# The first two pieces of x and the first weight granule's halves: two transfers instead of four

## The chip, the cores and the metric

The kernel runs on one core of one Trainium2 chip. The metric is device time in microseconds for one execution of the whole program. Times are medians over several executions; the profile is of one further execution, with its own time.

A core has several engines that run side by side, each with its own instruction queue worked off in order: PE (TensorE, matrix products; PEld is its weight load), DVE (VectorE), ACT (ScalarE), POOL (GpSimd) and SP (SyncE, here the queue that issues most transfers from memory). [...] The transfers themselves run on 16 DMA engines.

## The reference

The input is 512 tokens of 1024 channels in float32. Two layers each apply a gated feed-forward block, a mixer and a second feed-forward block, and a last normalization follows:

```python
for l in range(DEPTH):                                   # DEPTH = 2
    x = x + 0.5 * swiglu(rms_norm(x, ffn1_norm[l]), ffn1_w_in[l], ffn1_w_out[l])
    x = x + mixer(rms_norm(x, mix_norm[l]), ...)         # neighbourhood attention + 2-D DFT, gated
    x = x + 0.5 * swiglu(rms_norm(x, ffn2_norm[l]), ffn2_w_in[l], ffn2_w_out[l])
return rms_norm(x, final_norm)
```

with `swiglu(x, w_in, w_out) = (silu(g) * u) @ w_out` and `g, u` the two halves of `x @ w_in`; `w_in` is 1024 x 5632, `w_out` 2816 x 1024. Only the very first steps of the first `swiglu` matter for this change.

## The kernel before, in words

**Products in three parts.** Every float32 operand is split into a rounded high part and the low rest. For the weights ScalarE writes `whi` (L210, or L205 with the sign turned) and VectorE the rest `wlo` (L213, L206). For x they are `xh` (L353) and `xl` (L354). A product is then three matmuls per 128 rows of depth: `whi,xh` (L539), `whi,xl` (L540) and `wlo,xh` (L542). The root mean square is not needed for that: only the gain `gn` is multiplied into x; the division comes later. Most large products further on use Strassen's scheme of seven products, for which sums and differences of operand blocks are made.

**Weights come in granules.** A granule is 128 x 1024 float32, 512 KB. A list of items, one per granule and use, sets their order. `Item.load` issues the transfer on SP (L155) into a `raw` buffer, `Item.prep` makes `whi` and `wlo` of it; `ws.fetch` and `ws.next` keep loads and preparations ahead of the products. In the feed-forward stages the `raw` buffers are a pool of nine that are taken in turn. When a stage ends, the pool is closed, and the next stage's tiles take over its memory, each as soon as its last user there is done. Some loads are sums that POOL's queue adds in flight (L165).

**The start.** The first 256 gate and 256 up columns are computed plainly (the `cl` products): four granules, each of two 128-row pieces of depth, against the eight pieces of transposed x (`xt`, 128 channels x 512 tokens, 256 KB each). Per piece there are four output banks and so twelve matmuls. The first granule is loaded and prepared in two halves of 256 KB, so that PE can begin on the first piece of x with the first half. Before that, ten matmuls on zeros (`warm`, L143) run on PE. Each piece of x is also multiplied by the gain into `xr` (L428, two halves of 256 tokens), and halves are combined (L726 and later) for the Strassen products behind.

**What sets the order.** SP's order at the start is written out by hand (a block in which SP keeps program order): first piece of x, first weight halves, second piece of x, then x in pairs of pieces, each with the next granule. The order on PE, VectorE and ScalarE in this stretch is set by the framework's planner from dependences and its own estimates, apart from the combinations, which are by hand. POOL's first transfer of the mixer is `ch` (L1145), into memory of the closed `raw` pool.

Of the kernel before, what the change touches and what calls it, by code (L numbers as in the profile page):

```python
# [9 lines left out]
F32 = mybir.dt.float32  # L10
# [4 lines left out]
AF = mybir.ActivationFunctionType  # L15
ALU = mybir.AluOpType
AX = mybir.AxisListType

P = 128
D = 1024  # L20
T = 512
# [28 lines left out]
def _granules():  # L50

    names, at = [], {}

    def put(*key):
        at[key] = len(names)
        names.append(key)

    for l in range(L):
        for w in (1, 2):
            s = (l, w)  # L60
            for g in range(4):
                put(s, *(("cl", g) if s == (0, 1) else ("h" + "abcd"[g], 0, 0)))
            for j in range(NB):
                for g in range(2):
                    put(s, "a", j, g)
                for g in range(2):
                    put(s, "c", j, g)
                    put(s, "d", j, g)
                for g in range(2):
                    put(s, "b", j, g)  # L70
            for q in "abcd":
                for c in range(3):
                    for g in range(2):
                        put(s, "o" + q, c, g)
            if w == 1:
                s = (l, 0)
                for q in "abcd":
                    for g in range(2):
                        put(s, "u" + q, 0, g)
                for name, n in (("qk", 8), ("f", 5)):  # L80
                    for g in range(n):
                        put(s, name, g)
                for i in range(2):
                    for g in range(2):
                        put(s, "n", i, g)
                    for q in "acdb":
                        for g in range(2):
                            put(s, "g" + q, i, g)
                for q in "acdb":
                    for g in range(2):  # L90
                        put(s, "w" + q, 0, g)
    return names, at


GRAN, GRAN_AT = _granules()
# [1 line left out]

@with_exitstack
def encoder_kernel(
    ctx: ExitStack, tc: tile.TileContext, xin, xtr, wst, gains, gfin, gbias, bias_in, dft, chan, ident_in, rot, out  # L100
):
    nc = tc.nc
    V, S, G, PE = nc.vector, nc.scalar, nc.gpsimd, nc.tensor
# [11 lines left out]
    def nm(s):  # L115
        uid[0] += 1
        return f"{s}_{uid[0]}"

    def slot(dt=F32, s="k", shape=(4, 256)):
        return kp.tile([P, *shape], dt, tag="k", name=nm(s), bufs=23)  # L120
# [14 lines left out]
    ident = cp.tile([P, P], F32, tag="ident", name="ident")  # L135
# [31 lines left out]
    class Item:  # L167
# [30 lines left out]
        def prep(self, nxt):  # L198
            n = self.raw.n
            hi = wp.tile([P, 1024], F32R, tag="whi", name=nm("whi"), bufs=3)[:, 0:n]  # L200
            lo = wp.tile([P, 1024], F32R, tag="wlo", name=nm("wlo"), bufs=3)[:, 0:n]
            t = self.raw.t
            self.summed()
            if self.neg:
                S.activation(hi, t, AF.Copy, scale=-1.0)  # L205
                self.last = V.scalar_tensor_tensor(lo, t, -1.0, hi.bitcast(F32), ALU.mult, ALU.subtract)  # L206
            else:
                for c in range(0, n, n // self.parts):
                    cs = slice(c, c + n // self.parts)
                    S.activation(hi[:, cs], t[:, cs], AF.Copy)  # L210
                    if nxt and not nxt.twice:
                        nxt.summed()
                    self.last = V.tensor_tensor(lo[:, cs], t[:, cs], hi[:, cs].bitcast(F32), ALU.subtract)  # L213
            if self.then:
                G.dma_start(out=t, in_=wst[GRAN_AT[self.then]][:, 0:n], accum_op=ALU.add)
            self.out = (hi, lo)
# [123 lines left out]
    ws = Stream()  # L340
# [1706 lines left out]
    swap_pools(0, False)  # L2047
    norm = Norm(0)
    with tc.manual_schedule(engines={mybir.EngineType.SP}):
        for kts in ((0,), (1,), (2, 3), (4, 5), (6, 7)):  # L2050
            src = slot(F32, "xt", (2, T))[:, 0 : len(kts), :]
            nc.sync.dma_start(out=src, in_=xtr[:, kts[0] : kts[-1] + 1, :])
            ws.fetch(kts[-1] // 2 + 1)
            for k, kt in enumerate(kts):
                norm.given(*divmod(kt, 4), src[:, k, :])
        ws.fetch(6)
        for tb in range(TB):
            nc.sync.dma_start(out=x[:, tb, :], in_=xin[:, tb, :])
        nc.sync.dma_start(out=ident, in_=ident_in)
        ws.fetch(10)  # L2060
    for l in range(L):
        nxt = Norm(3 * l + 1)
        stage_ffn(norm, nxt, False)
        norm, nxt = nxt, Norm(3 * l + 2)
        stage_mixer(l, norm, nxt)
        norm, nxt = nxt, Norm(3 * l + 3)
        stage_ffn(norm, nxt, l == L - 1)
        norm = nxt
# [184 lines left out]
```

## Time and profile before

| | us |
|---|---|
| median of 3 runs | 1838.45 |
| lowest, highest | 1838.39, 1839.38 |
| the profiled execution's own time | 1837.46 |
| its span, first to last instruction | 1835.7 |
| PE busy in the span | 1823.8 |
| VectorE busy | 1607.2 |
| ScalarE busy | 1306.2 |

A row of a timeline reads: start in us from the span's start, time in us, engine, line, operation, output<-inputs, the number of instructions merged in the row, and in brackets how long the engine had been idle before and what ended that. "SPq" is the time that SP's queue spends on issuing a transfer, not the transfer's. In the chain of waits each row has start, time and what the end of the program depended on. In the table of stretches each engine has its busy time and instruction count; the last three columns are PE's granted clock, the mean busy share of the DMA engines and GB/s.

### The profile page before, as it was taken

The numbers are of one execution on the slowest core, as the hardware profiler recorded it, in microseconds if no ns is written. First come the engines' busy times: TensorE is split into PE (matmuls) and PEld (weight loads), VectorE is DVE, ScalarE is ACT, GpSimd is POOL, SyncE is SP. The second block draws the span as 40 slices with busy tenths as digits, with TensorE's granted clock in tenths as the row PEclk, the third lists the DMA queues.
The fourth block names the chain that finished last, engine by engine and source line by source line (L and its number), as shares of the span: only waits on it lengthen the run. The fifth ranks groups of instructions, "written<-read, shape, count | busy, mean of one in ns | idle before, by whom it ended". The sixth has DMA issues, their size and how long they took to land.

```text
span 1835.7 us, 24504 instructions
## 1 busy us (share of the span) xinstructions
PE 1823.8 (99%) x8766; PEld 1509.6 (82%) x8766; DVE 1607.2 (88%) x1952; ACT 1306.2 (71%) x1771; POOL 179.2 (10%) x219
## 2 busy tenths in 40 slices
PE   9999999999999999999999999999999999999998
PEld 7888888887878888888888888888888788888876
DVE  7878899878989988889998888998789899887898
ACT  6777875667576777787667777766776776777865
POOL 0001011110111010101010100101001111100010
PEclk9999999999999999999999999999999999999999
DMA  9898798963997789879878987998639876988795
GB/s 303 223 237 225 184 274 272 225 175 116 277 221 193 166 233 242 208 201 281 249 194 212 240 212 197 274 296 186 179 134 264 227 190 183 238 212 223 202 272 162
DMA packets 206387, 403.75 MB, mean 220 GB/s; under 512 B 108733, under 2 KB 108893, under 8 KB 206265
## 3 DMA queue, kind: packets, MB, share of 16 engines
q1 hardware_dynamic: 176536, 300.52, 51.0%
q0 software_dynamic: 29296, 101.12, 30.5%
q8 instruction: 69, 1.13, 0.3%
q10 hardware_dynamic: 432, 0.55, 0.1%
q14 instruction: 54, 0.43, 0.1%
HBM read 370.67 MB, written 2.11 MB: 203 GB/s over the span
## 4 chain that ended last, share of the span: by engine, by line
PE 89%; DVE 3%; DMA 3%; issue 2%; ACT 2%; POOL 0%; SPq 0%; DVEq 0%; ACTq 0%; POOLq 0%
PE A L539 10%; PE A L540 10%; PE A L542 10%; PE o L540 7%; PE o L539 7%; PE o L542 7%; PE B L542 5%; PE B L540 5%; PE B L539 5%; PE ps L344 3%; PE ps L345 3%; PE ps L346 2%; PE C L540 2%; PE C L539 2%; PE C L542 2%
## 5 line engine op out<-in xcount | busy, mean ns | idle before, releaser
L213 DVE TENSOR_TENSOR wlo<-raw,whi 128x1024 fp32r<-128x1024 f32 (+1 forms) x534 | 630.8, 1190 | 166.3 <-ACT whi L210 165.8
L210 ACT ACTIVATE whi<-raw 128x1024 fp32r<-128x1024 f32 (+1 forms) x534 | 546.2, 1033 | 265.4 <-DVE raw L182 70.7
L165 POOL DMA_DIRECT2D raw<-in_wst_dram x170 | 148.6, 900 | 1301.7 <-DMA raw<-in_wst_dram 467.6
L182 DVE TENSOR_TENSOR raw<-raw,raw 128x1024 f32<-128x1024 f32 (+1 forms) x148 | 176.1, 1190 | 2.0
L540 PE MATMUL A<-whi,xl 128*128 128x512 f32 x400 | 155.7, 389 | 0.0
L539 PE MATMUL A<-whi,xh 128*128 128x512 f32 x400 | 155.7, 389 | 0.0
L394 ACT ACTIVATE at<-zt 128x1024 uint16<-128x1024 uint16 (+2 forms) x96 | 110.2, 1165 | 12.0 <-DMA zt<-zs 12.0
L542 PE MATMUL A<-wlo,xh 128*128 128x512 f32 x400 | 115.0, 389 | 0.0
L205 ACT ACTIVATE whi<-raw 128x1024 fp32r<-128x1024 f32 (+1 forms) x83 | 85.6, 1036 | 38.7 <-issue 11.3
L206 DVE SCALAR_TENSOR_TENSOR wlo<-raw,whi 128x1024 fp32r<-128x1024 f32 (+1 forms) x83 | 98.6, 1192 | 11.5 <-ACT whi L205 11.5
L542 PEld LDWEIGHTS A<-wlo,xh 128*128 128x128 f32 x400 | 75.1, 188 | 15.6
L540 PEld LDWEIGHTS A<-whi,xl 128*128 128x128 f32 x400 | 75.1, 188 | 15.4
L539 PEld LDWEIGHTS A<-whi,xh 128*128 128x128 f32 x400 | 75.1, 188 | 15.4
L539 PE MATMUL B<-whi,xh 128*128 128x512 f32 x208 | 81.4, 391 | 1.2 <-ACT whi L210 1.1
L540 PE MATMUL B<-whi,xl 128*128 128x512 f32 x208 | 81.0, 390 | 0.0
L540 PE MATMUL C<-whi,xl 128*128 128x512 f32 x208 | 81.0, 389 | 0.0
L539 PE MATMUL C<-whi,xh 128*128 128x512 f32 x208 | 81.0, 389 | 0.0
L794 ACT ACTIVATE th<-sn,rh 128x512 f32<-128x512 f32 x80 | 54.9, 715 | 36.3 <-DVE sn L631 35.5
L375 ACT ACTIVATE zs<-th 128x1024 uint16<-128x1024 uint16 x80 | 79.5, 1043 | 0.9 <-DVE th L801 0.9
L626 ACT ACTIVATE sn<-A 128x512 f32<-128x512 f32 x104 | 59.0, 586 | 27.5 <-PE A L542 27.2
L542 PE MATMUL B<-wlo,xh 128*128 128x512 f32 x208 | 60.2, 391 | 0.2
L542 PE MATMUL C<-wlo,xh 128*128 128x512 f32 x208 | 60.1, 390 | 0.0
(451 smaller groups left out, 4618.7 us busy)
## 6 DMA issues: line engine op xcount, KB each, us to landing
raw<-in_wst_dram SPq DMA_DIRECT2D x468, 512.0 KB, 6.3
raw<-in_wst_dram POOLq DMA_DIRECT2D x180, 512.0 KB, 8.1
bm<-in_bias_dram SPq DMA_DIRECT2D x16, 512.0 KB, 6.2
raw<-in_wst_dram SPq DMA_DIRECT2D x30, 256.0 KB, 5.1
vs<-v SPq DMA_DIRECT2D x24, 128.0 KB, 5.8
x<-in_xin_dram SPq DMA_DIRECT2D x4, 512.0 KB, 10.2
raw<-in_wst_dram POOLq DMA_DIRECT2D x8, 256.0 KB, 8.4
dft<-in_dft_dram POOLq DMA_DIRECT2D x8, 256.0 KB, 6.7
```

Source lines behind the costliest of these rows:

```text
L165: G.dma_start(out=self.t, in_=wst[GRAN_AT[self.plus]][:, 0 : self.n], accum_op=ALU.add)
L182: V.tensor_tensor(self.raw.t, self.raw.t, self.add.t, ALU.add)
L205: S.activation(hi, t, AF.Copy, scale=-1.0)
L206: self.last = V.scalar_tensor_tensor(lo, t, -1.0, hi.bitcast(F32), ALU.mult, ALU.subtract)
L210: S.activation(hi[:, cs], t[:, cs], AF.Copy)
L213: self.last = V.tensor_tensor(lo[:, cs], t[:, cs], hi[:, cs].bitcast(F32), ALU.subtract)
L375: S.activation(s[:, h], words[:, h], AF.Copy)
L394: S.activation(to[:, w], t[:, w], AF.Copy)
L539: PE.matmul(ps, lh, rh, start=start, stop=False, skip_group_check=again)
L540: PE.matmul(ps, ll, rh, start=False, stop=False, skip_group_check=again)
L542: PE.matmul(ps, lh, rl, start=False, stop=stop, skip_group_check=again)
L626: last_snap[0] = S.activation(t[:, b, :], ps[b], AF.Copy)
```

## The change

The host lays the first two pieces of x and the two halves of the first granule side by side in a new input `head` (128 x 2 x 2 x 512: per piece, x and then its half of the weights). Two transfers of 512 KB bring them into two `xt` tiles. The first item's `raw` is then no buffer of the pool but a list of the two weight parts of these tiles, and `prep` takes its source from there. The input `xtr` holds the other six pieces.

```diff
-                    S.activation(hi[:, cs], t[:, cs], AF.Copy)
+                    src = t[c // T] if isinstance(t, list) else t[:, cs]
+                    S.activation(hi[:, cs], src, AF.Copy)
                     if nxt and not nxt.twice:
                         nxt.summed()
-                    self.last = V.tensor_tensor(lo[:, cs], t[:, cs], hi[:, cs].bitcast(F32), ALU.subtract)
+                    self.last = V.tensor_tensor(lo[:, cs], src, hi[:, cs].bitcast(F32), ALU.subtract)
...
     with tc.manual_schedule(engines={mybir.EngineType.SP}):
-        for kts in ((0,), (1,), (2, 3), (4, 5), (6, 7)):
-            src = slot(F32, "xt", (2, T))[:, 0 : len(kts), :]
-            nc.sync.dma_start(out=src, in_=xtr[:, kts[0] : kts[-1] + 1, :])
+        begin = [slot(F32, "xt", (2, T)) for _ in range(2)]
+        ws.items[0].raw.t = [t[:, 1, :] for t in begin]
+        for kt, t in enumerate(begin):
+            nc.sync.dma_start(out=t, in_=head[:, kt])
+            norm.given(0, kt, t[:, 0, :])
+        ws.fetch(1)
+        for kts in ((2, 3), (4, 5), (6, 7)):
+            src = slot(F32, "xt", (2, T))
+            nc.sync.dma_start(out=src, in_=xtr[:, kts[0] - 2 : kts[-1] - 1, :])
             ws.fetch(kts[-1] // 2 + 1)
             for k, kt in enumerate(kts):
                 norm.given(*divmod(kt, 4), src[:, k, :])
...
+    head = np.stack([xtr[:, 0:2], wst[GRAN_AT[(0, 1), "cl", 0]].reshape(P, 2, T)], axis=2)
+    xtr = np.ascontiguousarray(xtr[:, 2:])
```

How the instructions stand on the engines before and after follows for three places. Lines of the changed kernel lie one to seven further down (L354 is now the `xh` line, L211 `whi`, L214 `wlo`, L355 `xl`, L429 `xr`).

SP's first transfers before, from the program's start on; `xt` are pieces of x, `raw` is weights:

```order
L2052 DMA xt_102<-in_xtr_dram 128x512
L155 DMA raw_104<-in_wst_dram 128x512 x2
L2052 DMA xt_115<-in_xtr_dram 128x512
L2052 DMA xt_121<-in_xtr_dram 128x1024
L155 DMA raw_123<-in_wst_dram 128x1024
L2052 DMA xt_133<-in_xtr_dram 128x1024
```

And in the changed kernel:

```order
L2054 DMA xt_102<-in_head_dram 128x1024
L2054 DMA xt_103<-in_head_dram 128x1024
L2059 DMA xt_118<-in_xtr_dram 128x1024
L155 DMA raw_120<-in_wst_dram 128x1024
L2059 DMA xt_130<-in_xtr_dram 128x1024
```

The two weight halves and the single pieces are gone as transfers of their own; everything behind stands two places earlier.

VectorE from the low rest of the third granule's weights to that of the first Strassen weights, before (`wlo_227` is of the fourth `cl` granule, L726 a combination of `xr` halves):

```order
L213 TENSOR_TENSOR wlo_199<-raw_135,whi_198 128x1024
L726 TENSOR_TENSOR xr_111<-xr_111,xr_113 128x1024
L354 SCALAR_TENSOR_TENSOR xl_138<-xt_149,gn,xh_137 128x512
L428 TENSOR_SCALAR xr_141<-xt_149,gn 128x256
L428 TENSOR_SCALAR xr_143<-xt_149,gn 128x256
L354 SCALAR_TENSOR_TENSOR xl_138<-xt_149,gn,xh_137 128x512
L428 TENSOR_SCALAR xr_141<-xt_149,gn 128x256
L428 TENSOR_SCALAR xr_143<-xt_149,gn 128x256
L213 TENSOR_TENSOR wlo_227<-raw_151,whi_226 128x1024
L206 SCALAR_TENSOR_TENSOR wlo_255<-raw_161,whi_254 128x1024
```

And in the changed kernel, where `wlo_224` is of the fourth granule and the combination is L727:

```order
L214 TENSOR_TENSOR wlo_196<-raw_132,whi_195 128x1024
L429 TENSOR_SCALAR xr_138<-xt_146,gn 128x256
L355 SCALAR_TENSOR_TENSOR xl_135<-xt_146,gn,xh_134 128x512
L429 TENSOR_SCALAR xr_140<-xt_146,gn 128x256
L355 SCALAR_TENSOR_TENSOR xl_135<-xt_146,gn,xh_134 128x512
L429 TENSOR_SCALAR xr_138<-xt_146,gn 128x256
L429 TENSOR_SCALAR xr_140<-xt_146,gn 128x256
L214 TENSOR_TENSOR wlo_224<-raw_148,whi_223 128x1024
L727 TENSOR_TENSOR xr_109<-xr_109,xr_111 128x1024
L206 SCALAR_TENSOR_TENSOR wlo_252<-raw_158,whi_251 128x1024
```

The combination moved from ahead of the last x pieces to behind the fourth granule's low rest.

PE's first products of the second piece of x in the changed kernel (L540 is now `whi,xh`, L541 `whi,xl`; `cl` are the four output banks):

```order
L540 MATMUL cl_179<-whi_183,xh_105 128x512
L540 MATMUL cl_180<-whi_183,xh_105 128x512
L541 MATMUL cl_179<-whi_183,xl_106 128x512
L541 MATMUL cl_180<-whi_183,xl_106 128x512
L540 MATMUL cl_181<-whi_183,xh_105 128x512
L541 MATMUL cl_181<-whi_183,xl_106 128x512
```

Before, `whi,xh` and `whi,xl` alternated from the first bank on; now two `whi,xh` come first, for the first piece as well.

More of the change, by code (lines that the diff above doesn't have):

```diff
@@ L99, in encoder_kernel @@
 def encoder_kernel(
-    ctx: ExitStack, tc: tile.TileContext, xin, xtr, wst, gains, gfin, gbias, bias_in, dft, chan, ident_in, rot, out
+    ctx: ExitStack, tc: tile.TileContext, xin, head, xtr, wst, gains, gfin, gbias, bias_in, dft, chan, ident_in, rot, out
 ):
@@ L2240 @@
     nc = _bacc.Bacc("TRN2", target_bir_lowering=False, num_devices=1)
-    arrays = dict(xin=xin, xtr=xtr, wst=wst, gains=gains, gfin=gfin, gbias=gbias, bias=bias, dft=dft, chan=chan, ident=ident, rot=rot)
+    arrays = dict(xin=xin, head=head, xtr=xtr, wst=wst, gains=gains, gfin=gfin, gbias=gbias, bias=bias, dft=dft, chan=chan, ident=ident, rot=rot)
     arrays = {f"in_{k}_dram": v for k, v in arrays.items()}
```

## The prediction

> **What bounds the kernel now.** I read the page first, then the chain of waits, then the first 30 us engine by engine, because the transfers that change are the first ones of the program.
>
> ```profile
> span 1835.7 us, 24504 instructions
> PE 1823.8 (99%) x8766; PEld 1509.6 (82%) x8766; DVE 1607.2 (88%) x1952; ACT 1306.2 (71%) x1771; POOL 179.2 (10%) x219
> ```
>
> PE is busy for all but 11.9 us (1835.7 - 1823.8) of the span, so a change that removes no PE work can win only where PE waits or runs slowly. The chain of waits over the first 40 us shows who sets the pace there (start us, us, what):
>
> ```profile
> 2.61 6.61 DMA xt<-in_xtr_dram
> 9.24 0.88 DVE xr L428 x3
> ...
> 21.12 0.73 PE cl L542 x2
> ...
> 39.54 0.23 PE B L539
> ```
>
> First a transfer of x, then an unbroken run of VectorE, and from 21.12 us on PE itself. The timeline of PE (start us, us, what) shows what that costs PE:
>
> ```profile
> 1.19 4.45 PE L143 MATMUL ps<-warm 128*128 128x512 bf16 x10 [1.19 <-DVE ones L139]
> 5.14 0.92 PE L539 MATMUL cl<-whi,xh 128*128 128x512 f32 x1
> 5.87 0.63 PE L540 MATMUL cl<-whi,xl 128*128 128x512 f32 x1
> ...
> 6.72 0.42 PE L540 MATMUL cl<-whi,xl 128*128 128x512 f32 x1
> 6.98 0.40 PE L539 MATMUL cl<-whi,xh 128*128 128x512 f32 x1
> ...
> 8.83 0.39 PE L539 MATMUL cl<-whi,xh 128*128 128x512 f32 x1
> 9.18 0.50 PE L540 MATMUL cl<-whi,xl 128*128 128x512 f32 x1
> 9.51 0.39 PE L539 MATMUL cl<-whi,xh 128*128 128x512 f32 x1
> ...
> 11.81 0.39 PE L539 MATMUL cl<-whi,xh 128*128 128x512 f32 x1
> ...
> 20.65 0.39 PE L540 MATMUL cl<-whi,xl 128*128 128x512 f32 x1
> 21.12 0.73 PE L542 MATMUL cl<-wlo,xh 128*128 128x512 f32 x2
> 21.69 0.39 PE L539 MATMUL cl<-whi,xh 128*128 128x512 f32 x1
> ...
> 25.78 0.39 PE L539 MATMUL cl<-whi,xh 128*128 128x512 f32 x1
> ...
> 28.50 0.39 PE L539 MATMUL A<-whi,xh 128*128 128x512 f32 x1
> ```
>
> Starts matter here, not durations, since matmuls overlap. Undisturbed, 12 matmuls take 28.50 - 25.78 = 2.72 us, 0.227 each. From 5.87 to 6.72 they start 0.43 apart (two steps), at about half that rate; from 6.98 at the full one. Twelve matmuls use one piece of x (128 rows) with its half of the first weight granule. The second twelve (8.83 to 11.81) take 2.98 us, 0.26 more than 2.72: 9.18 and 9.51 came late. Then PE loses 0.36 us more, around 21.12: 0.47 instead of 0.23 before it, 0.57 instead of 0.45 behind. Three things can be won: 0.26, 0.36, and part of the half-rate start. ScalarE and VectorE show what those waited for:
>
> ```profile
> 3.85 0.72 ACT L353 ACTIVATE xh<-xt,gn 128x512 fp32r<-128x512 f32 x1 [1.17 <-DMA gn<-in_gains_dram]
> 4.48 0.61 ACT L210 ACTIVATE whi<-raw 128x512 fp32r<-128x512 f32 x1
> 5.85 0.63 ACT L210 ACTIVATE whi<-raw 128x512 fp32r<-128x512 f32 x1 [0.76 <-DMA raw<-in_wst_dram]
> 7.61 0.73 ACT L353 ACTIVATE xh<-xt,gn 128x512 fp32r<-128x512 f32 x1 [1.13 <-DMA xt<-in_xtr_dram]
> ```
>
> ```profile
> 4.61 0.75 DVE L354 SCALAR_TENSOR_TENSOR xl<-xt,gn,xh 128x512 fp32r<-128x512 f32 x1
> 5.27 0.69 DVE L213 TENSOR_TENSOR wlo<-raw,whi 128x512 fp32r<-128x512 f32 x1
> ...
> 7.61 0.62 DVE L428 TENSOR_SCALAR xr<-xt,gn 128x256 f32<-128x256 f32 x2 [0.40 <-DMA xt<-in_xtr_dram]
> 8.37 0.75 DVE L354 SCALAR_TENSOR_TENSOR xl<-xt,gn,xh 128x512 fp32r<-128x512 f32 x1
> ...
> 16.33 1.22 DVE L726 TENSOR_TENSOR xr<-xr,xr 128x1024 f32<-128x1024 f32 x1
> 17.47 0.75 DVE L354 SCALAR_TENSOR_TENSOR xl<-xt,gn,xh 128x512 fp32r<-128x512 f32 x1
> ...
> 19.84 1.22 DVE L213 TENSOR_TENSOR wlo<-raw,whi 128x1024 fp32r<-128x1024 f32 x1
> ```
>
> The first piece of x waits for the gains at 3.85, so it is itself in by then. Its weight half is in by 4.48 (ScalarE goes on without idle time), the second weight half at 5.85, the second piece of x at 7.61. The 9.18 matmul waited for the xl of 8.37 to 9.12, the 21.12 matmul for the wlo of 19.84 to 21.06.
>
> **The change, part by part.** (1) *Two issues fewer.* Four issues of 256 KB become two of 512 KB:
>
> ```profile
> 0.74 0.40 SPq L2052 DMA_DIRECT2D xt<-in_xtr_dram  x1
> 1.21 0.89 SPq L155 DMA_DIRECT2D raw<-in_wst_dram  x2
> ```
>
> An issue takes about 0.47 us of the queue (0.74 to 1.21), so everything from the third transfer on is issued about 0.9 us earlier. Bytes stay the same, and the stretches show what the DMA engines made of them (columns end with DMA share and GB/s):
>
> ```profile
> 2.00:4.00 2.00, 2.00 (x6) 0.76 (x5) 0.15 (x1) 0.82 (x3) 0.00 (x0) 1.00 0.89 301
> 4.00:6.00 2.00, 2.00 (x6) 1.06 (x5) 1.82 (x4) 1.24 (x3) 0.00 (x0) 1.00 0.78 210
> 8.00:10.00 2.00, 2.00 (x10) 1.35 (x9) 1.74 (x5) 1.10 (x3) 0.00 (x0) 1.00 1.01 399
> ```
>
> In the 4 to 6 us stretch they are idle 22% of the time. Earlier issues may fill that or not; no row says.
>
> (2) *The first pair is usable only when all of it is in.* Bounds: 3.8 us (the 524 KB and 25 KB of gains at 301 GB/s from 2.00 on) and 4.48 (the same bytes were in by then). I take 4.3, near the row that stands for the same bytes. ScalarE then makes xh (0.63 to the next start) and whi (0.61), so the first product can start at about 5.59 instead of 5.14. What hides this are the warm-up matmuls, which hold PE until 5.64 (1.19 + 4.45); the second product at 5.87 less 0.43 puts the first one's real start at 5.44. The delay is 0.15 us at half rate, worth 0.08 us of full-rate work (0.227/0.43). Bounds: nothing, and 0.17 (landing at 4.48). Without that cover it would be 0.45. VectorE's xl and wlo move by the same 0.45, to 5.06 and 5.72, and are needed only at the third and the ninth product.
>
> (3) *The second pair lands together.* At the earliest 4.3 + 524 KB at 399 GB/s = 5.6 us, at the latest 7.61, when the same bytes had landed; no row lies nearer to either, so I take the middle, 6.6. xh and whi are then done by 7.9 (0.63 + 0.61), xl by 8.11 (8.37 + 0.75 was 1.51 behind the landing), wlo by 8.71, all before PE comes to them at 8.91 (8.83 + 0.08). Even with 7.61 whi is done at 8.85 and xl at 9.12; the new order puts two whi,xh matmuls ahead of the first that needs xl, so that one stands at 8.91 + 0.45 = 9.36. The second twelve then take 2.72 us: 0.26 won.
>
> (4) *VectorE's order moves.* The combination of two xr halves (L726, 1.14 us from 16.33 to 17.47) now stands behind the wlo that PE awaited at 21.12. On the other side the second wlo half (0.6 to the next start: 1.81 - 1.22 for such a one and a long one, below at 309.96) comes behind the second xl instead of ahead. If the second pair lands at 7.61, VectorE starts the third piece at 9.63 instead of 9.24, and the wlo ends at 21.06 - 1.14 + 0.39 = 20.31; with 6.6 it is 1.0 us earlier still. PE comes for it at 20.65 + 0.23 - 0.18 = 20.70. So the 0.36 us go (bounds: 0 and 0.36). The moved combination feeds the product that starts at 39.54; it has over 15 us.
>
> (5) *The first granule takes no raw buffer*, which shifts the rotation of nine by one in this stage. At the entry of the mixer the ch transfer on POOL takes over the first buffer's place, and everything behind it on POOL waits:
>
> ```profile
> 307.63 1.22 DVE L213 TENSOR_TENSOR wlo<-raw,whi 128x1024 fp32r<-128x1024 f32 x1
> ...
> 309.96 1.81 DVE L213 TENSOR_TENSOR wlo<-raw,whi 128x1024 fp32r<-128x1024 f32 x2
> ```
>
> ```profile
> 309.14 0.57 POOL L1145 DMA_DIRECT2D ch<-in_chan_dram  x1 [20.65 <-DVE wlo L213]
> 312.15 0.85 POOL L165 DMA_DIRECT2D raw<-in_wst_dram  x1 [2.43 <-DMA raw<-in_wst_dram]
> ```
>
> Its releaser becomes the first of the pair at 309.96 (a 128x512, 0.69 us, done at 310.65), so ch goes out near 310.95 and is issued by 311.5. The next on POOL waits until 312.15 for its own data: nothing lost, with 0.63 us to spare. Beyond that, each us late would hold up POOL's loads by as much.
>
> Sum: +0.08 - 0.26 - 0.36 = **-0.54 us**; bounds -0.09 and -0.62. The profiled execution took 1837.46 us (span 1835.7 and 1.76 around it), which gives 1836.9. That execution lies 0.99 below the median of 1838.45 (runs from 1838.39 to 1839.38), so for the median I write **1837.9**. More than 0.62 cannot come from here, however early the data: before 5.44 PE is held by the warm-ups.
>
> [...]
>
> **Rivals.** *Slower: the clock rises later.* PE is at half rate up to 6.72, 5.6 us after its first warm-up. If the first pair lands after 4.35 (5.64 less the 1.29 it needs to become a product), PE stands idle between warm-ups and products, and the full rate may come later. Each us at half rate costs 0.47 us (1 - 0.227/0.43). The delay is bounded by nothing and by another 5.6 us; half of it costs 1.3, all of it 2.6. Time: 1837.9 + 1.3 = 1839.2, at most 1840.5. For it: my landing of 4.3 stands right at the edge. Against: a gap would be some tenths in over 4 us of work, and the gap before 21.12 left the rate as it was. Chance 0.12.
>
> [...]
>
> *The second pair lands late.* From 7.7 us on each us counts in full: at 8.5 the second twelve start at 9.79 instead of 8.91, the sum is +0.34, the time 1838.8. For it: the sag to 210 GB/s. Against: the same bytes had landed at 7.61 behind two more issues. Chance 0.08.
>
> *The gain is lost later: no change, 1838.45.* PE has 1% of idle time behind the start, and a wait there that isn't tied to PE's own progress would swallow half a us. Against: POOL's and SP's waits there end with VectorE's work, as above, and move along. Chance 0.10.
>
> *More than the sum*, by later waits that also shrink: 1836.5 or less; the 11.9 us of idle PE are the cap. Chance 0.05.
>
> **How the numbers follow.** The forecast keeps 0.65. Its own range is 1837.4 to 1838.9: the bounds of the sum and the spread of 0.99 us among the runs of before. With the clock and the late landing mostly in, I give 1836.9 to 1839.6 for 8 in 10. A change counts as faster or slower beyond 0.2%, 3.7 us, about what a measurement of this kernel can tell from no change. Every case above but its far tail lies inside: the clock rival ends at +2.1, the larger gain would have to take a third of all idle PE time. So 0.03 faster, 0.94 the same, 0.03 slower.
>
> **What would show it.** PE's timeline: first product near 5.6, half rate ending between 6.7 and 7.0, the second twelve without the 0.35 us steps, no gap at the first wlo pair near 20.7, and the A product starting near 27.96 instead of 28.50. ScalarE: the first xh at 4.3 (wrong if above 4.48), the second between 5.6 and 7.6. VectorE: no idle time from the third piece on, the L726 step (now L727) behind the fourth wlo. POOL: ch near 311, the raw transfer behind it still released by its data. Wrong would be a half-rate stretch that lasts to 8 us or more, a second pair after 7.7, or a difference beyond 1 us that arises after 30 us.

## The result and the profile after

The changed kernel took **1849.99 us** (median of 6 executions, 1844.04 to 1853.94), the kernel before beside it 1838.42 (six, 1837.50 to 1840.36): ratio 1.0057, 95% interval 1.0043 to 1.0072, slower by some 10 us. The prediction of 1837.9 was wrong. The profiled execution took 1848.69 us. Its page begins:

```profile
span 1846.9 us, 24498 instructions
PE 1828.4 (99%) x8766; PEld 1512.1 (82%) x8766; DVE 1606.5 (87%) x1952; ACT 1305.7 (71%) x1771; POOL 179.1 (10%) x219
```

PE's busy time grew by 4.6 us, its idle time from 11.9 to 18.5. Setting the same matmuls of both traces side by side tells where: the changed kernel is 1.7 us late at 30 us, still 1.8 at 480, 8.4 at 548, 9.1 at 1310 and 11.2 at the end. So there are two large losses: one at the start and, four times as large, one near 530 us, where the change edits nothing. The other 3 us come in small steps behind.

**The start.** ScalarE's timeline after (start us, us, what):

```profile
5.08 0.72 ACT L354 ACTIVATE xh<-xt,gn 128x512 fp32r<-128x512 f32 x1 [2.42 <-DMA xt<-in_head_dram]
5.71 0.61 ACT L211 ACTIVATE whi<-xt 128x512 fp32r<-128x512 f32 x1
6.30 0.72 ACT L354 ACTIVATE xh<-xt,gn 128x512 fp32r<-128x512 f32 x1
6.93 0.61 ACT L211 ACTIVATE whi<-xt 128x512 fp32r<-128x512 f32 x1
```

and PE's:

```profile
1.19 4.45 PE L143 MATMUL ps<-warm 128*128 128x512 bf16 x10 [1.19 <-DVE ones L139]
6.38 1.22 PE L540 MATMUL cl<-whi,xh 128*128 128x512 f32 x2 [0.74 <-ACT whi L211]
...
9.53 0.63 PE L541 MATMUL cl<-whi,xl 128*128 128x512 f32 x1
9.96 1.33 PE L543 MATMUL cl<-wlo,xh 128*128 128x512 f32 x4
11.13 0.62 PE L540 MATMUL cl<-whi,xh 128*128 128x512 f32 x2
...
30.19 0.39 PE L540 MATMUL A<-whi,xh 128*128 128x512 f32 x1
```

The first pair was usable only at 5.08, PE stood idle for 0.74 us behind the warm-ups, and its products started 0.43 us apart until about 10 us instead of 6.7. From the second pair on it went as forecast: nothing waits at 9.2, nor at the first `wlo` pair forecast near 20.7 (here at 22.94). VectorE's order there is the one forecast, the combination behind the fourth granule's low rest:

```profile
18.36 1.22 DVE L214 TENSOR_TENSOR wlo<-raw,whi 128x1024 fp32r<-128x1024 f32 x1
19.50 1.22 DVE L727 TENSOR_TENSOR xr<-xr,xr 128x1024 f32<-128x1024 f32 x1
```

The A product starts at 30.19 instead of 28.50.

**Near 530 us.** There the second gate block of the first mixer ends. SP issues two DMA transposes (`zs` to `zt`, L382), with two loads of weights between them; POOL issues two accumulating transfers (L216: b is added in flight to the d+a in a `raw` buffer), whose sums PE's next B product needs. The chain of waits of the changed kernel (start us, us, what):

```profile
510.18 15.65 issue
525.84 15.45 DMA raw<-in_wst_dram
541.37 1.06 ACT whi L211
```

ScalarE could take up the first of the two sums only at 541.37, 15.5 us after its issue. In the kernel before, POOL issued it at 523.77 and ScalarE took it up 9.6 us later:

```profile
523.77 0.86 POOL L215 DMA_DIRECT2D raw<-in_wst_dram  x1 [15.48 <-DVE wlo L213]
```

```profile
533.37 1.06 ACT L210 ACTIVATE whi<-raw 128x1024 fp32r<-128x1024 f32 x1 [0.42 <-DMA raw<-in_wst_dram]
```

The table of stretches (busy us and count per engine: PE, PEld, DVE, ACT, POOL; then granted clock, DMA share, GB/s) before:

```profile
525.00:530.00 5.00, 5.00 (x23) 4.01 (x23) 4.40 (x6) 2.80 (x4) 0.86 (x1) 1.00 1.40 218
530.00:535.00 5.00, 4.88 (x22) 3.71 (x21) 1.23 (x2) 4.01 (x4) 0.00 (x0) 1.00 0.98 197
535.00:540.00 5.00, 4.46 (x18) 3.04 (x18) 2.72 (x4) 3.12 (x3) 0.00 (x0) 1.00 1.00 380
```

and after:

```profile
525.00:530.00 5.00, 5.00 (x23) 4.15 (x23) 5.00 (x7) 3.04 (x4) 1.72 (x2) 1.00 1.08 286
530.00:535.00 5.00, 5.00 (x23) 3.98 (x23) 1.47 (x2) 4.24 (x5) 0.00 (x0) 1.00 1.32 39
535.00:540.00 5.00, 1.41 (x7) 0.83 (x5) 0.69 (x1) 0.03 (x1) 0.00 (x0) 0.95 1.28 108
540.00:545.00 5.00, 2.52 (x6) 2.06 (x7) 1.23 (x1) 1.06 (x1) 0.00 (x0) 0.50 1.00 290
```

This is how the late loss looks here: from 530 to 535 us the DMA share is 1.32 (the packets' times, added up, exceed the time of the 16 engines), and only 39 GB/s are moved. A high share alone is no sign of it: the kernel before had 1.40 from 525 to 530 us, at 218 GB/s. PE runs dry, and its granted clock then falls to 0.50. The DMA queues (packets, MB, share of 16 engines; q1 holds SP's transfers, the transposes among them, q0 POOL's) from 527 to 533 us before:

```profile
q0 software_dynamic: 165, 0.61, 95.7%
q1 hardware_dynamic: 1569, 0.40, 31.2%
```

and from 529.5 to 540.5 us after:

```profile
q1 hardware_dynamic: 1271, 0.35, 64.8%
q0 software_dynamic: 156, 0.61, 62.6%
```

By these shares a packet of q1, nearly all of 256 bytes, took 19 ns on average before (0.312 x 6 us x 16 / 1569) and 90 ns after; one of q0 0.56 us before and 0.71 after. So in this profile it was mainly the transposes that crawled while POOL's accumulating packets ran beside them.

### The profile page after: what moved, and what is told of

It reads as the page before. It is cut to its first block, busy times and chain, and to the rows that moved or that the text cites. A ratio compares the mean times of both kernels' runs of the same rounds, so it can differ in the third digit from the quotient of the medians.

```text
span 1846.9 us, 24498 instructions
## 1 busy us (share of the span) xinstructions
PE 1828.4 (99%) x8766; PEld 1512.1 (82%) x8766; DVE 1606.5 (87%) x1952; ACT 1305.7 (71%) x1771; POOL 179.1 (10%) x219
## 3 DMA queue, kind: packets, MB, share of 16 engines
q8 instruction: 69, 1.13, 0.3%
## 4 chain that ended last, share of the span: by engine, by line
PE 83%; DMA 7%; issue 4%; DVE 3%; ACT 2%; POOL 0%; DVEq 0%; ACTq 0%; SPq 0%; POOLq 0%
PE A L540 9%; PE A L541 9%; PE A L543 9%; PE o L543 7%; PE o L540 7%; PE o L541 7%; DMA raw<-in_wst_dram 7%; PE B L543 4%; PE B L540 4%; PE B L541 4%; PE ps L345 2%; PE ps L346 2%; PE ps L347 2%; PE C L541 2%; PE C L540 2%
## 5 line engine op out<-in xcount | busy, mean ns | idle before, releaser
L214 DVE TENSOR_TENSOR wlo<-raw,whi 128x1024 fp32r<-128x1024 f32 (+1 forms) x532 | 629.1, 1192 | 177.7 <-ACT whi L211 177.1
L211 ACT ACTIVATE whi<-raw 128x1024 fp32r<-128x1024 f32 (+1 forms) x532 | 544.8, 1034 | 267.5 <-DVE raw L182 68.4
L540 PE MATMUL A<-whi,xh 128*128 128x512 f32 x400 | 155.9, 390 | 0.0
L541 PE MATMUL A<-whi,xl 128*128 128x512 f32 x400 | 155.8, 390 | 0.0
L540 PE MATMUL B<-whi,xh 128*128 128x512 f32 x208 | 82.5, 397 | 7.1 <-ACT whi L211 7.0
L540 PEld LDWEIGHTS A<-whi,xh 128*128 128x128 f32 x400 | 75.1, 188 | 15.5
L541 PEld LDWEIGHTS A<-whi,xl 128*128 128x128 f32 x400 | 75.2, 188 | 15.3
L541 PE MATMUL B<-whi,xl 128*128 128x512 f32 x208 | 82.1, 395 | 0.0
L540 PE MATMUL C<-whi,xh 128*128 128x512 f32 x208 | 81.1, 390 | 0.0
L541 PE MATMUL C<-whi,xl 128*128 128x512 f32 x208 | 81.0, 390 | 0.0
## 6 DMA issues: line engine op xcount, KB each, us to landing
x<-in_xin_dram SPq DMA_DIRECT2D x4, 512.0 KB, 10.2
```

What stands on the lines that cost most here:

```text
L211: S.activation(hi[:, cs], src, AF.Copy)
L214: self.last = V.tensor_tensor(lo[:, cs], src, hi[:, cs].bitcast(F32), ALU.subtract)
L540: PE.matmul(ps, lh, rh, start=start, stop=False, skip_group_check=again)
L541: PE.matmul(ps, ll, rh, start=False, stop=False, skip_group_check=again)
```

## The experiments

Every group shared one chip and the runs of the kernel before on it. "Late" is the number of executions above 1845 us; it is a rough sign, since the start and small losses elsewhere add to it too.

### Placement, program, clock

**e1_layout**: the program of before on the arrays of the change (`head` and the shorter `xtr`), still four transfers.

```diff
-                    nc.sync.dma_start(out=self.t[:, cs], in_=wst[GRAN_AT[self.key]][:, cs])
+                    src = wst[GRAN_AT[self.key]][:, cs] if parts == 1 else head[:, c // T, 1, :]
+                    nc.sync.dma_start(out=self.t[:, cs], in_=src)
...
+            if len(kts) == 1:
+                nc.sync.dma_start(out=src, in_=head[:, kts[0], 0:1, :])
```

> The program of before (four transfers of 256 KB, its raw pool, its order), reading the first two pieces of x and the first weight granule's halves from the new array, and the rest from the shortened one: the placement of all inputs in memory is that of the change, nothing else is. Placement theory (the new and the shorter array shift the weights in memory, and their transfers run at another speed): the late loss of about 9 us near 530 us is there, the start is that of before: 1846 to 1849. Timing theory (the late loss follows from the late start): first xh near 3.85, first product near 5.1, offset under 0.3 us at 30 us and at 530 us, 1837.5 to 1839.5.

**e2_tail**: the changed program, but the inputs of before keep their places.

```diff
-            nc.sync.dma_start(out=src, in_=xtr[:, kts[0] - 2 : kts[-1] - 1, :])
+            nc.sync.dma_start(out=src, in_=xtr[:, kts[0] : kts[-1] + 1, :])
...
-    arrays = dict(xin=xin, head=head, xtr=xtr, wst=wst, gains=gains, gfin=gfin, gbias=gbias, bias=bias, dft=dft, chan=chan, ident=ident, rot=rot)
+    arrays = dict(xin=xin, xtr=xtr, wst=wst, gains=gains, gfin=gfin, gbias=gbias, bias=bias, dft=dft, chan=chan, ident=ident, rot=rot, head=head)
```

> The two transfers of the change, its order and its pools, but the new array is the last input and the transposed x keeps its full size, so that the inputs of before keep their places in memory. Placement theory: start as in the change (first xh near 5.1, full rate from 11 us, offset +1.7 us), no late loss: 1839.5 to 1841. Timing theory: the late loss returns, 1845 to 1854.

**e3_warm**: the changed kernel with 12 warm-up matmuls (below); **e4_cold**: the kernel before with `WARM = 3`.

```diff
-WARM = 10
+WARM = 12
```

> The changed kernel with 12 warm-up matmuls instead of 10, so that PE has no idle time before the first product (10 end near 5.44 at 0.43 us each, 12 near 6.3). Clock theory of the start (the 0.74 us of idle time kept PE at half rate up to 11 us): half rate ends near 7, the second twelve start near 9.4 instead of 11.1, offset to before at 30 us under 0.5 us. Rival (the rate rises some fixed time after the first real product): half rate to 11 us, offset 1.7 us as in the change. For the late loss, the timing theory expects none with the offset gone (1837.5 to 1840), the placement theory still 8 to 9 us (1846 to 1848).

> The kernel before with 3 warm-up matmuls instead of 10: PE idles from about 2.5 us to 5.1 us, transfers, placement and pools are those of before. Clock theory: half rate to about 10 us, 12 or more products at 0.43 us, offset at 30 us between +1 and +2.3 us. Timing theory of the late loss: with that offset 6 us or more are lost near 530 us too, 1845 to 1854. Placement theory: the offset stays as it is, 1839.5 to 1841.

| run | median us | lowest, highest | late | ratio to before, 95% interval |
|---|---|---|---|---|
| before, beside them | 1843.32 | 1838.90, 1856.35 | 13 of 31 | |
| e1_layout | 1846.12 | 1837.69, 1856.19 | 5 of 10 | 1.0011 (0.9984 to 1.0039) |
| e2_tail | 1844.41 | 1840.27, 1857.63 | 5 of 10 | 1.0017 (0.9994 to 1.0040) |
| e3_warm | 1842.85 | 1839.71, 1849.75 | 4 of 10 | 0.9999 (0.9982 to 1.0016) |
| e4_cold | 1847.92 | 1842.77, 1850.18 | 8 of 10 | 1.0002 (0.9979 to 1.0026) |

None of the theories survived in the form in which it was put. On this chip the kernel *before* spread over 17 us. In the profiled executions, e1, e2 and e3 lost nothing between 530 and 548 us against the profile of before, e4 lost 4.9 there and 3.9 more near 1445 us, where the second layer has the same step. So the late loss is something that comes or stays away from execution to execution, with either kernel. At the start the same program (e2) landed its first pair at 5.30 and yet was level with before at 30 us: its full rate began at 6.6 us, in spite of 0.96 us of idle time. e3 says little on the clock: its full rate came during the warm-ups, which therefore ended at 5.78 and left a gap of 0.86. e4, whose PE idled for 3.0 us ahead of its first product, was only 0.45 us behind at 30 us, where 1.0 to 2.3 were expected.

### Is the loss there again, and what makes it?

**e5_after**: the changed kernel, nothing edited.

> The changed kernel as it is, beside the kernel before on the same chip. In the four runs so far, kernels with either start lay anywhere between 1838 and 1858 us, the kernel before itself between 1838.9 and 1856.4. Theory of chance (the late loss is a collision of transfers near 530 us and near 1445 us that comes or stays away in each execution, with either kernel): both spread over more than 8 us, the medians lie within 3 us of each other, ratio 0.998 to 1.002. Theory of the change (its late start or its placement brings the loss on): the changed kernel stays 8 to 12 us above the kernel before, ratio 1.004 to 1.007.

**g1_before, g1_after**: the accumulating transfers held back on POOL until the second transpose has landed.

```diff
+                if just_turned:
+                    z = just_turned.pop()
+                    gated[:] = [G.dma_start(out=to, in_=z[0:1, 0, 0, 0:32].bitcast(F32)).ins]
+                with tc.issue_after(gated[0]) if gated else nullcontext():
                     G.dma_start(out=t, in_=wst[GRAN_AT[self.then]][:, 0:n], accum_op=ALU.add)
```

> The kernel before, with a small transfer that reads the second turned tile of the gate block on POOL's queue ahead of the two accumulating transfers near 524 us (and near 1434 us), so that these are issued only when the transposes have landed. Collision theory (the transposes crawl because accumulating transfers run beside them): no stretch with a DMA share of 1.2 or more at under 110 GB/s, spread under 5 us, median 1838 to 1843; a wait of 0 to 3 us at each of the two places in return. Rival (the loss comes from elsewhere, such as the speed of all transfers of an execution): spread as for the kernel before, over 10 us.

> The same gate in the changed kernel. If the collision is the whole late loss, this and the gated kernel before differ only by the start: from -0.7 to +1.7 us, median within 2 us of it, spread under 5 us. If the change itself brings a late loss: 6 us or more above the gated kernel before.

**n2_before**: plain transfers of the same bytes instead of the transposes. It leaves out the turning of the words, so what follows computes with other values.

```diff
-        nc.sync.dma_start_transpose(
-            out=t.rearrange("p h q (b t) -> p (h q b) t", b=2), in_=s.rearrange("p h q b f -> p (h q b f)")
-        )
+        nc.sync.dma_start(
+            out=t.rearrange("p h q t -> p (h q t)"), in_=s.rearrange("p h q b f -> p (h q b f)")
+        )
```

> The kernel before with plain transfers of the same bytes in place of the DMA transposes (the words are not turned, so what follows computes with wrong activations). Collision theory: without transposes there is nothing that crawls, spread under 5 us, 1835 to 1841. Rival (accumulating transfers jam by themselves, or all transfers are slow in some executions): spread over 10 us as before.

| run | median us | lowest, highest | late | ratio to before, 95% interval |
|---|---|---|---|---|
| before, beside them | 1839.43 | 1836.19, 1847.62 | 4 of 23 | |
| e5_after | 1844.60 | 1839.04, 1854.23 | 6 of 12 | 1.0022 (1.0000 to 1.0044) |
| g1_before | 1848.82 | 1847.12, 1852.50 | 6 of 6 | 1.0053 (1.0040 to 1.0066) |
| g1_after | 1851.15 | 1847.43, 1854.10 | 6 of 6 | 1.0061 (1.0047 to 1.0075) |
| n2_before | 1838.91 | 1836.11, 1841.51 | 0 of 11 | 0.9992 (0.9981 to 1.0004) |

Without transposes the spread shrinks to 5.4 us and none of the 11 executions is late. The gate ends the crawl as well: no stretch of 5 us of the two gated profiles, from 520 to 545 us or from 1425 to 1460, has a DMA share of 1.2 or more, and the gated kernels spread over 5.4 and 6.7 us. But its price was put far too low. POOL's queue and the chain of waits of g1_before:

```profile
530.05 0.53 POOL L219 DMA_DIRECT2D seen<-zt  x1 [19.44 <-DMA zt<-zs]
530.57 1.81 POOL L221 DMA_DIRECT2D raw<-in_wst_dram  x2
```

```profile
530.57 7.53 DMA raw<-in_wst_dram
```

The two transfers went out from 530.57 on instead of 523.77, and the sums were usable 7.5 us later: 3.9 us lost here and 7.3 in the second layer (5.6 and 7.0 in the profile of g1_after). All 12 gated executions took over 1847 us. e5_after is a new draw of the changed kernel: 6 of 12 late, and its profiled execution shows the loss (+7.5 us between 530 and 548) although it was 0.7 us *early* at 480. So a late start is not needed. Its start is nearly the forecast one (PE):

```profile
6.07 0.73 PE L540 MATMUL cl<-whi,xh 128*128 128x512 f32 x2 [0.43 <-ACT whi L211]
6.64 0.63 PE L541 MATMUL cl<-whi,xl 128*128 128x512 f32 x2
7.11 0.39 PE L540 MATMUL cl<-whi,xh 128*128 128x512 f32 x1
```

Here full rate ruled from the first products on, and the A product started at 27.97; the forecast was 27.96.

### The change without the collision

**n3_before, n3_after**: both kernels without transposes, side by side (the edit of n2_before).

> The kernel before without DMA transposes (plain transfers of the same bytes instead, the words not turned), once more, as the partner of the next run on the same chip. Collision theory: spread under 6 us, no run above 1843.

> The changed kernel without DMA transposes, in the same way. Theory of chance (the change does nothing to the late part but shift it): no late loss, and against its partner only the start counts, -0.7 to +1.7 us, median difference between -0.5 and +1.5 us. If the change itself makes later transfers slower: 5 us or more above its partner.

**f1_before, f1_after**: in the second gate block b is loaded into buffers of its own and added by VectorE, so that nothing accumulates beside the transposes.

```diff
-                    add(d, None if dma else b)
+                    add(d, Raw(b.key, b.n) if fresh else None if dma else b)
...
-                    add(d, a, then=b.key if dma else None)
+                    add(d, a, then=b.key if dma and not fresh else None)
...
-                strassen(s, lambda q: "g" + q, i, two, ORDER if i else FIRST, True, on_chip=False)
+                strassen(s, lambda q: "g" + q, i, two, ORDER if i else FIRST, True, on_chip=False, fresh=i == 1)
```

> The kernel before with the second gate block's sum d+a+b made on chip: b's two granules are loaded into buffers of their own by SP and added by VectorE, instead of being accumulated by POOL's transfers beside the transposes near 524 and 1434 us. Same bytes from memory, four VectorE additions of 1.21 us more, four accumulating transfers fewer. Theory that accumulating transfers beside transposes make the crawl: spread under 6 us, 1836 to 1842, at or below the best runs of the kernel before. Rival (transposes crawl beside any transfer): spread over 8 us as before. Cost if two buffers less of lookahead count: 1 to 4 us more in every execution.

> The same on-chip sum in the changed kernel. If accumulation beside transposes is the late loss: 1836 to 1843, within 1.5 us of its partner without the change, spread under 6 us. If the change brings a late loss of its own: 5 us or more above its partner.

| run | median us | lowest, highest | late | ratio to before, 95% interval |
|---|---|---|---|---|
| before, beside them | 1840.65 | 1836.35, 1857.17 | 5 of 34 | |
| n3_before | 1838.73 | 1835.84, 1841.81 | 0 of 12 | 0.9990 (0.9976 to 1.0004) |
| n3_after | 1838.84 | 1837.35, 1845.47 | 1 of 12 | 0.9990 (0.9976 to 1.0004) |
| f1_before | 1835.76 | 1833.24, 1839.64 | 0 of 12 | 0.9963 (0.9943 to 0.9983) |
| f1_after | 1836.01 | 1832.08, 1843.06 | 0 of 12 | 0.9970 (0.9954 to 0.9986) |

This settles two things. Taking away *either* partner, the transposes or the accumulation beside them, ends the late loss in both kernels: 1 of 59 executions of n2, n3 and f1 is late, beside 9 of 57 of the kernel before and 6 of 12 of the changed one (e5, on n2's chip). The one late execution, 1845.47 us of n3_after, was not profiled; the profiled one, 1844.06, lost nothing between 530 and 548 us. Some spread stays all the same: f1_after has 11 us, where under 6 was expected, by one execution of 1843.06 that no profile caught. And without the late loss the change is worth next to nothing: the medians differ by 0.1 us (n3) and 0.25 us (f1); the difference of the means is +1.0 and +0.1 us, each with a 95% interval of 1.9 us to either side (from the 12 and 12 times). f1 also beats the kernel before: 4.9 us below the median of before beside it, best execution against best execution 3.1 us. The stretches of f1_before show why:

```profile
530.00:535.00 5.00, 5.00 (x23) 4.12 (x22) 3.54 (x5) 5.00 (x6) 0.00 (x0) 1.00 1.01 397
535.00:540.00 5.00, 5.00 (x23) 4.13 (x22) 5.00 (x7) 4.78 (x5) 1.72 (x2) 1.00 0.75 193
```

The additions fall where VectorE had waited (3.54 us busy instead of 1.23 from 530 to 535), and PE no longer waits for the B product at all: 1.9 us less than the quiet profile of before between 530 and 548 us, 1.4 less between 1430 and 1460.

### Does the change bring the loss on?

**e6_after, e7_after**: the changed kernel twice more. **d1_late**: the kernel before with `WARM = 20`.

> The changed kernel unchanged, for the frequency of late losses, counted as executions above 1845 us. Theory of one distribution: about as often as the kernel before beside it (there so far 4 of 23, 5 of 34 and 13 of 31), 1 to 5 of 12, ratio 0.998 to 1.003. Theory of a higher frequency: 6 or more of 12 (so far 6 of 12), ratio above 1.002.

> The same kernel once more, on the same terms: 1 to 5 of 12 above 1845 us if the distribution is one, 6 or more if the change raises the frequency.

> The kernel before with 20 warm-up matmuls instead of 10: the first products are held back by some 2 to 3 us (the first ten end near 5.4 us, ten more at 0.227 to 0.43 us each), everything else is the kernel before. If a later start raises the frequency of the late loss: 6 or more of 12 above 1845 us. If not: as often as the kernel before, and the best executions 1 to 3 us above its best.

**e8_count**: the changed kernel with two small transfers more on SP's queue, which gives all later ones the place in SP's order that they have in the kernel before. **e8_layout** and **e8_tail** are e1_layout and e2_tail once more.

```diff
         ws.fetch(1)
+        for _ in range(2):
+            nc.sync.dma_start(out=small("dum"), in_=gains[:, 0:8])
```

> The changed kernel with two small transfers (128 rows of 32 bytes) more on SP's queue behind the first three, so that every later transfer has the same place in the order of SP's transfers and the same completion semaphore as in the kernel before. If the place in SP's order (two transfers fewer) makes the first transpose's issue longer: back to 3.6 to 4.1 us, 1 to 5 of 12 executions above 1845 us. If it is the placement of the inputs or something else: 4.3 us or more, 6 to 11 of 12.

> The program of before on the change's arrays, once more with 5 rounds. If the placement in memory raises the frequency: 6 or more of 12 above 1845 us and an issue of 4.3 us or more for the first transpose near 517 us. If not: 1 to 5 of 12 and about 4.0 us (its first run had 5 of 10 beside 13 of 31 of the kernel before, and 3.98 us).

> The changed program with the new array last and the transposed x whole, once more with 5 rounds. If the program alone raises the frequency: 6 or more of 12 above 1845 us and 4.3 us or more. If the placement is needed too: 1 to 5 of 12 and under 4.1 us (its first run had 5 of 10, and 3.75 us).

| run | median us | lowest, highest | late | ratio to before, 95% interval |
|---|---|---|---|---|
| before, beside the next three | 1841.51 | 1836.49, 1858.53 | 4 of 29 | |
| e6_after | 1849.87 | 1839.43, 1857.06 | 9 of 12 | 1.0038 (1.0014 to 1.0061) |
| e7_after | 1851.17 | 1843.77, 1855.66 | 11 of 12 | 1.0047 (1.0026 to 1.0068) |
| d1_late | 1844.01 | 1836.40, 1848.71 | 5 of 12 | 1.0003 (0.9978 to 1.0027) |
| before, beside the last three | 1843.41 | 1836.61, 1859.13 | 12 of 29 | |
| e8_count | 1845.11 | 1838.41, 1857.78 | 6 of 12 | 1.0013 (0.9983 to 1.0042) |
| e8_layout | 1848.18 | 1839.16, 1858.09 | 10 of 12 | 1.0032 (1.0011 to 1.0054) |
| e8_tail | 1845.79 | 1840.52, 1856.71 | 8 of 12 | 1.0015 (0.9989 to 1.0040) |

The theory of one distribution falls. The changed kernel was late in 31 of 42 executions (5 of 6, then 6, 9 and 11 of 12), the kernel before in 38 of 152 (8 of the 58 beside them), and the share differs from chip to chip (from 4 of 29 to 13 of 31 for the kernel before). Its start does not explain that: with the bound at 1847 us, higher by more than the late start costs, it is 26 of 42 against 26 of 152 (4 of 58). In the mean the changed kernel took 4.4, 7.4 and 8.5 us more than the kernel before beside it (e5, e6, e7). But no part of the change could be named as the cause. Placement alone gave 15 of 22, the program alone 13 of 22, the restored count of transfers 6 of 12; and the late start of d1 5 of 12, where before had 4 of 29. All kernels other than the two compared that keep the transposes and the ungated accumulation (e1 to e4, d1, e8) together were late in 51 of 88, the kernel before beside them in 29 of 89. Above 1847 us it is 33 against 21, and d1 and e8_tail started 1.7 and 1.8 us later in their profiles. So whether nearly any edit makes late executions more frequent is not shown; that this change does is.

What the profiles do show is a sign that goes ahead of the loss. Relative to the start of the first transpose's issue, SP's loads of the 18 us ahead of it and POOL's accumulating transfers (6.36 and 8.09 us behind it) stand at the same place in all these kernels to 0.01 us. What differs is how long the issue takes. (POOL's last plain load lies 6.7 to 10.7 us ahead, in no order that goes with the loss.) SP's queue before:

```profile
517.41 4.08 SPq L381 DMA_TRANSPOSE zt<-zs  x1
521.58 1.00 SPq L155 DMA_DIRECT2D raw<-in_wst_dram  x2
522.63 4.41 SPq L381 DMA_TRANSPOSE zt<-zs  x1
```

and in e8_layout:

```profile
517.09 4.77 SPq L382 DMA_TRANSPOSE zt<-zs  x1
521.95 0.99 SPq L156 DMA_DIRECT2D raw<-in_wst_dram  x2
523.00 5.52 SPq L382 DMA_TRANSPOSE zt<-zs  x1
```

The second transpose starts 5.22 us behind the first in the one and 5.91 in the other, and so runs further into the sums at 6.36. The time of that issue, and what each profiled execution lost between 530 and 548 us against the first profile of before:

| issue of the first transpose, us | execution: loss, us |
|---|---|
| 3.64 to 4.08 | e4 4.9; e2 -1.2; d1 -1.4; e8_tail 0.5; e3 0.0; e1 -1.1; before 0 |
| 4.30 to 4.77 | after 6.3; e7 8.8; e5 7.5; e6 12.7; e8_count 8.3; e8_layout 18.4 |

All six with the long issue lost 6 us or more, six of the seven with the short one at most 0.5. (The gated kernels, and those without accumulation or transposes there, are left out.) The expectations of the three e8 runs had named 4.1 and 4.3 us as the bounds, and these runs fall on either side as the others do. The same pair of transposes stands in the second layer, near 1430 us: there its first issue took 3.06 to 3.78 us in all thirteen profiles, and only e4 (3.56) lost more than 1.4 us between 1430 and 1460. So the exception is e4, twice. e8_tail is also a warning on the count: its profiled execution is late (1845.64 us) with 0.5 us lost here. e1 and e8_layout are the same kernel, at 3.98 and 4.77: the issue is no property of the program alone. The worst one, e8_layout:

```profile
530.00:535.00 5.00, 4.02 (x18) 2.98 (x16) 0.69 (x1) 2.63 (x3) 0.00 (x0) 1.00 1.31 52
535.00:540.00 5.00, 0.00 (x0) 0.00 (x0) 0.00 (x0) 0.00 (x0) 0.00 (x0) 0.68 1.48 45
540.00:545.00 5.00, 0.00 (x0) 0.00 (x0) 0.00 (x0) 0.00 (x0) 0.00 (x0) 0.50 1.07 78
```

Whether the long issue makes the jam or is its first symptom, why it is long, and why so often with the changed kernel, stays open. No run separates an earlier state of the DMA queues from a later one.

## Why the prediction was wrong, point by point

- **"The forecast"** (1837.9) missed by 12 us. In the profiled execution the start accounts for 2.2 of it (the A product at 30.19 where 27.96 was forecast), the loss near 530 us for 6.6. That loss is no term of the sum and no rival: the range puts everything behind the start at the spread of three runs, and the text ahead of the prediction says that only the very first steps matter. But near 524 us two kinds of transfer stand side by side that jammed in some executions (39 GB/s at a DMA share of 1.32 in the changed kernel's profile). The step that failed is the bound "the spread of 0.99 us among the runs of before": three runs within 1 us were taken as the kernel's spread. The same kernel later spread over 11 to 23 us in each of five groups. The prediction named the marker, "a difference beyond 1 us that arises after 30 us", but its rivals there, with chances of 0.10 and 0.05, were a gain that gets lost or grows, not a loss.
- **Part 1, issues**: right. The second piece's pair led to `xh` at 6.01 to 6.62 us in ten profiled executions with two transfers, against 6.88 to 7.88 in nine with four. From 4 to 10 us the DMA engines moved over 400 GB/s in the changed kernel's profile (406, 420 and 424 in its three stretches of 2 us), without the sag to 210.
- **Part 2, the first pair**: mis-sized. Taken 4.3, bounds 3.8 and 4.48; measured 4.78 to 5.48 (ten executions, median 5.1), where four transfers gave 3.85 to 4.78 (nine, median 4.4). The upper bound was one execution's row ("the same bytes were in by then"), and that execution was the earliest of the nine. The lower bound set the pair's 549 KB, gains included, against all that the DMA engines move, as if nothing else were under way. But from 1 to 5 us the ten executions moved 832 to 942 KB (the GB/s of four stretches of 1 us, added up), bytes of the later transfers among them; and in six of the ten ScalarE's wait ended with the gains, not with the pair. Part of the lateness seems to go with the new array rather than with merging: from 1 to 4 us the ten moved 419 to 524 KB, the seven with four transfers and the old arrays 558 to 641, and e1 and e8_layout, with four transfers out of `head`, 486 and 451 (first `xh` at 4.53 and 4.78). The cover failed with it: PE stood idle 0.43 to 1.35 us ahead of the first product in all ten.
- **Parts 3 and 4**: right. The second twelve run dense (11.13 to 13.87, 2.74 us), and the gap at the `wlo` pair is gone (its two matmuls take 0.45 us, from 22.94 to 23.39, instead of 0.57).
- **Part 5, `ch`**: right that it costs nothing (it was issued at 308.07, and its successor on POOL waited for its own data), wrong in its place (near 311) and its releaser:

```profile
308.07 0.57 POOL L1146 DMA_DIRECT2D ch<-in_chan_dram  x1 [17.94 <-DVE raw L182]
314.26 0.85 POOL L165 DMA_DIRECT2D raw<-in_wst_dram  x1 [5.63 <-DMA raw<-in_wst_dram]
```

- **The rival "the clock rises later"** (chance 0.12) came true in four of the ten two-transfer executions (after, e6, f1_after, e8_tail): their A product starts at 30.22 on average, in the other six at 28.28, and in the seven with four transfers and ten warm-ups at 28.33. So it costs 1.9 us, within the bounds of 1.3 and 2.6, and the start as a whole is worth about +0.7 (0.4 x 1.9 and -0.05 else) where -0.54 was forecast. Its condition was wrong, though: idle time alone didn't decide. e7 had 1.35 us of it and e2 0.96, and both ran at full rate from their first products on. The four late ones have 16 or 17 half-rate steps, the six others 8 or 9. Eight steps more at 0.43 us instead of 0.227 make 1.6 us, an estimate from these traces that comes near the 1.9. The granted clock's record of 1.00 begins at 10.2 to 10.6 us in the four, at 4.5 to 6.3 in the six; what decides when it begins, no run shows.
- **"The second pair lands late"** did not happen (all by 6.62, the limit was 7.7). **"The gain is lost later"** named waits that aren't tied to PE; where it was lost was not a wait that swallows half a us but transfers that ran slowly side by side (a packet of q1 took 90 ns instead of 19, one of q0 0.71 us instead of 0.56).

## What to carry to other kernels

Before a forecast of half a us, ask how far the kernel's own executions spread; three runs lay within 0.99 us here, and the same kernel later spread over 11 to 23. Look for places where a DMA transpose and an accumulating transfer are issued within a few us of each other (here the sums 6.36 and 8.09 us behind the first transpose) and PE waits for the sum: in this kernel a sum on VectorE, in its idle time, took away both the jam and the ordinary wait (ratio 0.9963, interval 0.9943 to 0.9983). With the first transfers merged, the first piece was usable 0.7 us later in the median (5.1 instead of 4.4 us; part of it perhaps from the new array alone), and the warm-up matmuls did not cover that: PE stood idle 0.43 to 1.35 us. When a landing is forecast from a rate, count the bytes of the transfers issued behind too: from 1 to 5 us 832 to 942 KB were moved here, and the pair with the gains is 549.

## What the runs showed of the hardware that was not expected

- Transposes beside accumulating transfers: the small packets of q1 took 90 ns each on average in the changed kernel's profile (529.5 to 540.5 us), 19 in the quiet one of before (527 to 533). Each of the seven profiles with a loss has a stretch of 5 us between 530 and 540 us with a DMA share of 1.2 to 1.7 and only 34 to 98 GB/s. At such a share the quiet profiles of e8_tail and of before moved more: 149 GB/s at 1.22 (530 to 535 us) and 218 at 1.40 (525 to 530). Where the transposes ran beside plain loads, in f1's two profiles, no such stretch is seen: 181 to 302 GB/s at a share of 1.02 to 1.13 between 520 and 530 us.
- The issue of one and the same DMA transpose on SP took 3.64 to 4.77 us in different executions; the long ones preceded the jam.
- The long stall was paid for again: the B product of the changed kernel started 8.0 us late, and its delay grew to 9.6 us within its first matmuls, while the granted clock was 0.50 (stretch from 540 to 545 us); by 550 us it was back to 8.6.
- The share of late executions of one unchanged kernel was 13 of 31, 4 of 23, 5 of 34, 4 of 29 and 12 of 29 in five groups on five chips.
